# Down projection of a two-layer decoder trunk: seven of eleven row pairs by seven products in all four SwiGLU halves, every second pair's weight sums made by DMA, a larger descriptor store for GpSimd's transfers

## The chip, the cores and the metric

The kernel runs on one core of a Trainium2 chip. The metric is device time in microseconds (us) for one execution; of several executions the median counts. The core has five engines that run in their own order and meet at semaphores: PE (TensorE, matmuls; its weight loads are listed as PEld), DVE (VectorE), ACT (ScalarE), POOL (GpSimd), and SP, which issues most DMAs. [...]

## The reference

Input `x` is 256 tokens by 1024 channels, float32. The trunk has two layers, each of which is: a SwiGLU half step, a mixer (attention), a SwiGLU half step; a final RMSNorm ends it. A half step is

```python
def swiglu(h, w_gate, w_up, w_down):
    return (jax.nn.silu(h @ w_gate) * (h @ w_up)) @ w_down
h = h + 0.5 * swiglu(rmsnorm(h, g), w_gate, w_up, w_down)
```

`w_gate` and `w_up` are 1024 x 2816, `w_down` is 2816 x 1024. There are four such half steps: f10 and f20 in layer 0 (before and after its mixer a), f11 and f21 in layer 1 (before and after its mixer b). The change lies in them.

## The kernel before

**Number format.** Each float32 factor is split into a high part (ScalarE copy into fp32r, tiles `wh`) and a low part (VectorE subtraction, tiles `wl`), and a product is three matmuls: high x high, high x low, low x high (`product`, lines 185 to 192: L188, L190, L192). In the gate and up products of a half step two of the three share one weight load (L199, L205). So every weight that is multiplied passes ACT once and DVE once.

**A half step.** `ffn_blocks` goes over the 22 blocks of 128 hidden channels, two blocks f, f+1 per 1 MB tile of each of `w_gate` and `w_up` (`unit`: load into one of four `raw` buffers by SP, split by ACT L176 and DVE L177 into eight `wh` and eight `wl` buffers). f10's first four blocks are computed by `opening` while the first weights arrive. `close` evaluates silu(gate) x up and keeps each block's activation, split, until the down projection.

**The down projection** (`quartered`) multiplies activations (256 tokens x 2816) by `w_down`. It takes the 22 blocks in 11 pairs 0 to 10. A pair is a 2 x 2 problem: two halves of the tokens (128 each), two blocks of the contraction, two halves of the output (512 columns each).

- A *plain* pair makes all eight products, that is 24 matmuls of 128 x 512.
- A *fast* pair (its number is in `sums`) makes seven products, 21 matmuls, in the manner of Strassen and Winograd (`fast`). It needs four sums of the activations (*left* sums) and four sums of the pair's four weight blocks, a, b, c, d (*right* sums).
- Pairs 9 and 10 are held back and multiplied at the end, output quarter by quarter (`close`).

The left sums are made by `quarter_sums` in the gate and up part, as soon as both blocks of the pair are there: one 256-column and two 128-column VectorE operations (L412 to L414) and a split of the result (ACT L99, DVE L96). They stay in borrowed buffers named in `HOMES`.

The right sums come in one of two ways.

- *By VectorE*: `load` adds in SBUF, one 1024-column operation (tile `sum_..ac`, L655) and two 512-column ones (`sum_..bd`, L656, L657) for each pair. The pair needs one load of 1 MB.
- *By DMA* (pairs in `kept`): `right_sums` lets POOL copy and add rows of `w_down` in HBM, while the gate and up part runs: six calls one after the other, copy a and c, add to both, copy b from a, add, copy d from b, add; each for four pairs in transfers of two pairs (512 KB), 16 transfers in all (L579 copies, L584 adds). Each call is tied to a block of activations by a small POOL copy (L588), so the six are spread over six steps of the loop over f. The pair then needs two raw buffers and 1.75 MB of loads by SP: three of its own blocks and the 1 MB of sums (L640, L641, L643).

In both ways seven weight blocks of 128 x 512 are split by ACT (L633) and DVE (L634), for a plain pair four.

| half step | fast pairs before | of these, sums by DMA | sums by VectorE |
|---|---|---|---|
| f10 | 1 2 4 6 7 | none | 1 2 4 6 7 |
| f20 | 1 to 6 | 1 2 3 4 | 5 6 |
| f11 | 1 2 3 4 6 | 1 2 3 4 | 6 |
| f21 | 1 to 6 | 1 2 3 4 | 5 6 |

**Order of the work.** The program's text gives the data flow; a planner in the framework chooses, when the program is built, the order in which each engine's queue takes its instructions, so that instructions of neighbouring steps are interleaved on DVE and ACT. Each engine then runs its queue strictly in order. The buffers limit how far the supplying engines run ahead of PE: four `raw`, eight `wh` and eight `wl` (a fast pair takes four of each). The tiles `xx0` to `xx3` hold the normalised input of the gate and up part and are free for other use when PE's last gate and up product is done.

**Other names the change touches.** `rotate` (L809 to L817) applies the rotary embedding in the mixers with two temporaries, `rota` and `rotb`, two buffers each. `qkl` holds low parts of queries and keys in the mixers, and the `sum_..ac` tiles in the down projections. `dynamic_dma_scratch_size=1024` (in `kernel`) is the store for descriptors of POOL's transfers.

Of the kernel before, what the change touches and what calls it, by code (L numbers as in the profile page):

```python
# [26 lines left out]
ROT = 16  # L27
# [40 lines left out]
def trunk(ctx: ExitStack, tc: tile.TileContext, a: dict, out: bass.AP):  # L68
    nc = tc.nc
# [112 lines left out]
    def rows(w, k0, k, c0, n):  # L182
        return w[k0 * P:(k0 + k) * P, c0:c0 + n].rearrange("(k p) n -> p k n", p=P)
# [365 lines left out]
    def left_sums(pairs, homes):  # L549

        sums = {}
        assert len(pairs) <= len(homes)
        for i, home in zip(pairs, homes):
            if home in ("mk", "gf"):
                parts = xp.tile([P, 2, 512], F32R, tag=home, name=f"left_{i}")
                sums[i] = (parts[:, 0], parts[:, 1])
            elif home == "qkh":
                parts = ap_.tile([P, 2, 512], F32R, tag=home, name=f"left_{i}", bufs=2)
                sums[i] = (parts[:, 0], parts[:, 1])
            elif home == "pT":  # L560
                sums[i] = tuple(pp.tile([P, 512], F32R, tag=home, name=f"left_{i}_{j}") for j in range(2))
            else:
                sums[i] = tuple(xp.tile([P, 512], F32R, tag=f"{home[:2]}{int(home[2]) + j}", name=f"left_{i}_{j}")
                                for j in range(2))
        return sums

    latest = []

    def right_sums(name, w, first, m, places):


        kept = aside.tile([P, m, 4, 512], F32, tag=f"right_{name}", name=f"right_{name}")
        src = w[2 * first * P:2 * (first + m) * P, :].rearrange("(i k p) (c n) -> k c p i n", k=2, p=P, n=512)
        a, c, d, b = [kept[:, :, j] for j in range(4)]

        def copy(*moves):
            for to, of in moves:
                for i in range(0, m, 2):
                    nc.gpsimd.dma_start(to[:, i:i + 2], of[:, i:i + 2])  # L579

        def add(*moves):
            for to, of in moves:
                for i in range(0, m, 2):
                    nc.gpsimd.dma_start(to[:, i:i + 2], of[:, i:i + 2], accum_op=ALU.add)  # L584

        def paced(call):
            scrap = sp.tile([P, 1], F32, tag="scrap", name="scrap")
            mark = nc.gpsimd.tensor_copy(scrap, latest[-1][:, 0, 0:1].bitcast(F32))  # L588
            with tc.issue_after(mark.ins):
                call()  # L590

        calls = [lambda: copy((a, src[0, 0]), (c, src[1, 1])), lambda: add((a, src[0, 1]), (c, src[0, 1])),
                 lambda: copy((b, a)), lambda: add((b, src[1, 1])), lambda: copy((d, b)), lambda: add((d, src[1, 0]))]
        return {first + i: kept[:, i] for i in range(m)}, {at: lambda call=call: paced(call) for at, call in zip(places, calls)}

    def together(*tables):
        calls = [dict(enumerate(t)) if not isinstance(t, dict) else t for t in tables]

        def run(f):
            for t in calls:  # L600
                if f in t:
                    t[f]()

        return [lambda f=f: run(f) for f in range(KF // 2)]

    def ffn(name, layer, which, norm, after, first=None, beside=(), homes=HOMES, fast=(), queue=(), kept={}, calls={}):
        wg, wu, wd = (a[f"ffn{which}_w_{n}"][layer] for n in ("gate", "up", "down"))
        sums = left_sums(fast, homes)
        blocks = ffn_blocks(name, wg, wu, norm, first, together(beside, calls), sums, queue)
        if which == 1:  # L610
            table(AF.Exp, blocks[-1][:, 0, 0:1].bitcast(F32))
        down(f"{name}_d", wd, blocks, sums, kept, norm.halved(), after)


    def quartered(name, w, acts, sums, kept, collected, tail=2):
# [21 lines left out]
        def load(i):  # L637
            raw = rawp.tile([P, 4, 512], F32, tag="raw", name=f"raw_{name}_{i}")
            if i in kept:
                nc.sync.dma_start(raw[:, :2], rows(w, 2 * i, 2, 0, 512))  # L640
                nc.sync.dma_start(raw[:, 2], w[(2 * i + 1) * P:(2 * i + 2) * P, 512:])  # L641
                right = rawp.tile([P, 4, 512], F32, tag="raw", name=f"raw_{name}_{i}r")
                nc.sync.dma_start(right, kept[i])  # L643
                b11, b21 = split(f"{i}a", raw[:, :2])
                b22, = split(f"{i}b", raw[:, 2:3])
                ta, tc = split(f"{i}c", right[:, :2])
                td, tb = split(f"{i}d", right[:, 2:])
                return b11, b21, b22, ta, tc, tb, td
            nc.sync.dma_start(raw.rearrange("p (k c) n -> p k (c n)", k=2), rows(w, 2 * i, 2, 0, D))
            if i not in sums:  # L650
                return split(f"{i}a", raw[:, :2]) + split(f"{i}b", raw[:, 2:])
            n = sorted(set(sums) - set(kept)).index(i) % 4
            ac = ap_.tile([P, 2, 512], F32, tag="qkl", name=f"sum_{name}_{i}ac", bufs=2)
            bd = xp.tile([P, 2, 512], F32, tag=f"xx{n}", name=f"sum_{name}_{i}bd")
            nc.vector.tensor_add(ac, raw[:, 0::3], raw[:, 1:2].to_broadcast([P, 2, 512]))  # L655
# [151 lines left out]
    def rotate(v, t, name):  # L807

        n = v.shape[1]  # L809
        cs = rot[:, t, 0:1, :].to_broadcast([P, n, ROT])  # L810
        sn = rot[:, t, 1:2, :].to_broadcast([P, n, ROT])
        ta = sp.tile([P, n, ROT], F32, tag="rota", name=f"ra_{name}", bufs=2)
        tb = sp.tile([P, n, ROT], F32, tag="rotb", name=f"rb_{name}", bufs=2)
        nc.vector.tensor_mul(ta, v[:, :, :ROT], cs)
# [189 lines left out]
    n0, n1, n2 = Norm(0, "n0"), Norm(1, "n1"), Norm(2, "n2")  # L1004
    n3, n5, n6 = Norm(4, "n3"), Norm(5, "n5"), Norm(6, "n6")

    kept_f10, calls_f10 = {}, {}
    ffn("f10", 0, 1, n0, n1, first, fast=(1, 2, 4, 6, 7), kept=kept_f10, calls=calls_f10)
    nc.sync.dma_start(rot, a["rot"].rearrange("t p c n -> p t c n"))
    mask = load_mask(0)  # L1010
    xs = n1.xs()
    w, n = a["a_w_qkv"][0], HG * DH
# [7 lines left out]
    def ending(at, apart=2.6):  # L1020
# [3 lines left out]
          [steps(0, 3.0, 11.0, 14.5, 16.5, 19.3), steps(1, 3.0, 11.0, 13.8, 16.5, 19.3), steps(2, 4.0),  # L1024
           [(3.4, "s", (6, 7))] + ending(8.4)],
          a["a_w_o"][0], mask, n2, {3: 4, 4: 5})
    kept_f20, calls_f20 = right_sums("f20_d", a["ffn2_w_down"][0], 1, 4, (1, 2, 3, 4, 5, 6))
    ffn("f20", 0, 2, n2, n3, fast=(1, 2, 3, 4, 5, 6), queue=(6, 7) + (LAST_O,) * 6, kept=kept_f20, calls=calls_f20)
    kx = []
    kept_f11, calls_f11 = right_sums("f11_d", a["ffn1_w_down"][1], 1, 4, (1, 2, 3, 4, 5, 6))  # L1030
    ffn("f11", 1, 1, n3, n5, homes=HOMES[:5], fast=(1, 2, 3, 4, 6),
        beside=[lambda k=k: kx.append(gain(k, 3, "kx", "kx")) for k in range(KD)], kept=kept_f11, calls=calls_f11)
    mask = load_mask(1)
    xkv, xq = by_token(kx), n5.xs()
# [7 lines left out]
          a["b_w_o"][0], mask, n6)  # L1042
    gfin = xp.tile([P, D], F32, tag="gf", name="gfin")
    nc.sync.dma_start(gfin, a["final_norm"].rearrange("(o d) -> o d", o=1).to_broadcast([P, D]))
    kept_f21, calls_f21 = right_sums("f21_d", a["ffn2_w_down"][1], 1, 4, (1, 2, 3, 4, 5, 6))
    sums = left_sums((1, 2, 3, 4, 5, 6), ("mk", "kx4", "kx6", "qkh", "qkh", "pT"))
    h = [[xp.tile([P, 512], F32, tag=f"kx{2 * t + c}", name=f"h_{t}_{c}") for c in range(2)] for t in range(NT)]

    def turn_h(t, c):
        tr = trt(f"h_{t}_{c}")  # L1050
        for k in range(4):
# [5 lines left out]
                        queue=(4, 5, 6, 7) + (LAST_O,) * 4)  # L1057
# [68 lines left out]
```

## Time and profile before

| | |
|---|---|
| time, median of 3 runs (lowest, highest) | 961.97 us (961.61, 962.04) |
| the profiled execution | 962.21 us |
| its span in the trace | 960.4 us |
| granted TensorE clock | 0.999 |
| bytes read from and written to HBM | 208.60 MB, 26.21 MB |

The profile's page has six parts: busy time per engine, the span in 40 slices, DMA queues, the chain of work that ended last, the costliest groups of instructions, and the DMA issues. A group's line gives source line, engine, operation, output<-input, shape and count, then busy time and the mean duration, then the idle time before it and what released it. Timeline rows give the start, the duration, engine and line of an instruction. A row of the view by windows gives a stretch, its length, busy time (and number of instructions) of PE, PEld, DVE, ACT and POOL, the granted clock, the mean busy share of the 16 DMA engines, and GB/s. Durations of successive instructions overlap a little; the distance of starts is what an instruction costs in a full queue.

### The profile page before, as it was taken

What the parts mean: (1) busy time and instruction counts of PE and PEld (TensorE: products, weight loads), DVE (VectorE), ACT (ScalarE), POOL (GpSimd) and SP (SyncE); (2) the same over time, 40 slices, a digit from 0 to 9 for tenths busy, and PEclk for the clock granted to TensorE, in tenths of its full rate; (3) what the DMA queues carried; (4) which work ended last, traced back from release to release, by engine and by line L of the source; (5) the groups of instructions that cost most, each with busy time, mean ns of one, the idle gap of its engine ahead of it and who ended that gap; (6) DMA issues with size and microseconds to landing.
All of it is one profiled execution on the core that took longest, in us unless ns stands there. A gap on an engine that the chain in (4) does not pass through costs nothing.

```text
span 960.4 us, 14716 instructions
## 1 busy us (share of the span) xinstructions
PE 952.6 (99%) x5337; PEld 824.8 (86%) x5337; DVE 802.4 (84%) x1463; ACT 640.6 (67%) x1151; POOL 148.0 (15%) x178
## 2 busy tenths in 40 slices
PE   9999999999999999999999999999999999999997
PEld 7888888888899888888888888888888988888886
DVE  7998889878878888779789986887788789887796
ACT  7866567666867666667586666766577777765661
POOL 0100000022620312100023210000251322120000
PEclk9999999999999999999999999999999999999999
DMA  9785546565235799948849997784624449997661
GB/s 327 245 263 175 177 158 235 201 203 175 93 128 179 256 266 270 318 168 298 260 143 327 276 314 222 273 315 150 245 97 168 132 133 288 262 305 218 232 228 45
DMA packets 138906, 210.61 MB, mean 219 GB/s; under 512 B 4689, under 2 KB 104529, under 8 KB 137297
## 3 DMA queue, kind: packets, MB, share of 16 engines
q1 hardware_dynamic: 128128, 183.58, 56.4%
q0 software_dynamic: 9984, 25.17, 11.5%
q8 instruction: 42, 0.69, 0.3%
q10 hardware_dynamic: 720, 0.92, 0.3%
q14 instruction: 32, 0.25, 0.1%
HBM read 208.60 MB, written 26.21 MB: 244 GB/s over the span
## 4 chain that ended last, share of the span: by engine, by line
PE 98%; DVE 1%; DMA 0%; ACT 0%; issue 0%; POOL 0%; SPq 0%; POOLq 0%; DVEq 0%; ACTq 0%
PE f_g L199 17%; PE f_u L199 17%; PE f_u L205 9%; PE f_g L205 9%; PE dn_f_d L192 6%; PE dn_f_d L190 6%; PE dn_f_d L188 6%; PE dn_f_d_m L192 2%; PE dn_f_d_m L188 2%; PE dn_f_d_m L190 2%; PE qk_a L188 2%; PE qk_a L192 2%; PE qk_a L190 2%; PE v_a L188 1%; PE ot_ao L781 1%; PE ot_ao L783 1%
## 5 line engine op out<-in xcount | busy, mean ns | idle before, releaser
L199 PE MATMUL f_g<-x_n,wh_f_g 128*128 128x512 f32 x672 | 175.8, 393 | 0.0
L199 PE MATMUL f_u<-x_n,wh_f_u 128*128 128x512 f32 x672 | 173.3, 390 | 0.0
L199 PEld LDWEIGHTS f_u<-x_n,wh_f_u 128*128 128x128 f32 x672 | 126.1, 188 | 26.6
L199 PEld LDWEIGHTS f_g<-x_n,wh_f_g 128*128 128x128 f32 x672 | 121.2, 189 | 22.3
L177 DVE TENSOR_TENSOR wl_f_g<-raw_f_g,wh_f_g 128x1024 fp32r<-128x1024 f32 x84 | 101.3, 1219 | 16.9 <-PE f_g L205 15.7
L177 DVE TENSOR_TENSOR wl_f_u<-raw_f_u,wh_f_u 128x1024 fp32r<-128x1024 f32 x84 | 102.5, 1220 | 2.7 <-ACT wh_f_u L176 2.7
L205 PE MATMUL f_u<-x_n,wl_f_u 128*128 128x256 f32 x672 | 101.1, 283 | 0.0
L205 PE MATMUL f_g<-x_n,wl_f_g 128*128 128x256 f32 x672 | 100.5, 282 | 0.0
L205 PEld LDWEIGHTS f_g<-x_n,wl_f_g 128*128 128x128 f32 x672 | 94.2, 190 | 6.1
L176 ACT ACTIVATE wh_f_g<-raw_f_g 128x1024 fp32r<-128x1024 f32 x84 | 87.6, 1052 | 9.1 <-PE f_g L199 5.0
L205 PEld LDWEIGHTS f_u<-x_n,wl_f_u 128*128 128x128 f32 x672 | 89.6, 192 | 0.0
L176 ACT ACTIVATE wh_f_u<-raw_f_u 128x1024 fp32r<-128x1024 f32 x84 | 86.5, 1049 | 2.2 <-PE dn_f_d L192 2.1
L438 ACT ACTIVATE j_f_g<-j_f_g 128x256 f32<-128x256 f32 x88 | 36.2, 417 | 55.0 <-DVE j_f_g L437 53.8
L403 ACT ACTIVATE j_f_g<-f_g 128x256 f32<-128x256 f32 x88 | 33.1, 377 | 27.1 <-PE f_g L205 26.9
L403 ACT ACTIVATE j_f_u<-f_u 128x256 f32<-128x256 f32 x88 | 33.5, 381 | 21.4 <-PE f_u L205 21.3
L301 POOL TENSOR_TENSOR d_n<-w_n,expo 128x8 f32<-128x8 f32 x4 | 7.6, 1898 | 260.4 <-DVE w_n L297 260.4
L584 POOL DMA_DIRECT2D right_f_d<-in_ffn_w_down_dram x24 | 28.0, 1165 | 119.4 <-issue 90.7
L404 DVE TENSOR_TENSOR j_f_g<-f_g,j_f_g 128x256 f32<-128x256 f32 x88 | 37.1, 421 | 7.5 <-ACT j_f_g L403 7.4
L857 POOL TENSOR_SCALAR sm_a<-sm_a,ls_a 128x128 f32<-128x128 f32 (+1 forms) x32 | 32.8, 1044 | 44.1 <-DVE ls_a L855 44.1
L404 DVE TENSOR_TENSOR j_f_u<-f_u,j_f_u 128x256 f32<-128x256 f32 x88 | 37.0, 421 | 0.8 <-ACT j_f_u L403 0.5
L99 ACT ACTIVATE x_n<-gains_hT 128x256 fp32r<-128x256 f32 x48 | 21.7, 500 | 23.6 <-DVE gains_hT L734 23.0
L437 DVE TENSOR_TENSOR j_f_g<-j_f_g,r_n 128x256 f32<-128x256 f32 x88 | 36.5, 421 | 0.4
(690 smaller groups left out, 2369.5 us busy)
## 6 DMA issues: line engine op xcount, KB each, us to landing
raw_f_g<-in_ffn_w_gate_dram SPq DMA_DIRECT2D x42, 1024.0 KB, 5.9
raw_f_u<-in_ffn_w_up_dram SPq DMA_DIRECT2D x42, 1024.0 KB, 6.5
raw_f_d<-in_ffn_w_down_dram SPq DMA_DIRECT2D x32, 1024.0 KB, 6.3
right_f_d<-in_ffn_w_down_dram POOLq DMA_DIRECT2D x36, 512.0 KB, 7.8
raw_qka<-in_a_w_qkv_dram SPq DMA_DIRECT2D x16, 512.0 KB, 4.4
right_f_d<-right_f_d POOLq DMA_DIRECT2D x12, 512.0 KB, 7.7
raw_f_d<-in_ffn_w_down_dram SPq DMA_DIRECT2D x12, 512.0 KB, 4.3
raw_va<-in_a_w_qkv_dram SPq DMA_DIRECT2D x4, 1024.0 KB, 5.7
```

The lines of the kernel that those rows point to most:

```text
L176: nc.scalar.activation(wh, r, AF.Copy)
L177: nc.vector.tensor_sub(wl, r, wh.bitcast(F32))
L188: nc.tensor.matmul(ac, xh, wh, start=first, stop=False)
L190: nc.tensor.matmul(ac, xh, wl, start=False, stop=False)
L192: nc.tensor.matmul(ac, xl, wh, start=False, stop=last)
L199: nc.tensor.matmul(ac, wh, flat(x), start=first and i == 0, stop=False)
L205: nc.tensor.matmul(ac[:, :S], wl, x[:, 0, :], start=False, stop=last and i == len(ws) - 1)
L403: nc.scalar.activation(s, ac[:, S:], AF.Copy)
L404: nc.vector.tensor_add(s, ac[:, :S], s)
L437: nc.vector.tensor_mul(g, g, norm.row)
L438: nc.scalar.activation(g, g, AF.Silu)
L857: nc.gpsimd.tensor_scalar(sm[:, seg], sm[:, seg], ls[:, t:t + 1], None, op0=ALU.mult)
```

## The change

- Pairs 1 to 7 are fast in all four half steps. That makes six plain pairs fast: 3 and 5 in f10, 7 in f20, 5 and 7 in f11, 7 in f21.
- The right sums of pairs 1, 3, 5, 7 come by DMA in all four (`right_sums` with a step of two pairs); those of 2, 4, 6 by VectorE. f10 gets a set of 16 transfers by POOL that it did not have, one step of the loop later than the others (places 2 to 7).
- Both VectorE sums of a pair now lie in `xx` tiles, alternately `xx0`, `xx1` and `xx2`, `xx3`. `qkl` is taken for two left sums in f11 and one in f21.
- `rota` and `rotb` have one buffer each. The descriptor store is 2048 bytes.

```diff
-            elif home == "qkh":
+            elif home in ("qkh", "qkl"):
                 parts = ap_.tile([P, 2, 512], F32R, tag=home, name=f"left_{i}", bufs=2)
...
-    def right_sums(name, w, first, m, places):
+    def right_sums(name, w, first, m, places, step=1):
         kept = aside.tile([P, m, 4, 512], F32, tag=f"right_{name}", name=f"right_{name}")
-        src = w[2 * first * P:2 * (first + m) * P, :].rearrange("(i k p) (c n) -> k c p i n", k=2, p=P, n=512)
+        rows_of = w[2 * first * P:, :].rearrange("(i k p) (c n) -> k c p i n", k=2, p=P, n=512)
+        src = [[rows_of[k, c][:, :(m - 1) * step + 1:step] for c in range(2)] for k in range(2)]
...
-                    nc.gpsimd.dma_start(to[:, i:i + 2], of[:, i:i + 2])
+                    nc.gpsimd.dma_start(to[:, i:min(i + 2, m)], of[:, i:min(i + 2, m)])
...
-        return {first + i: kept[:, i] for i in range(m)}, {at: lambda call=call: paced(call) for at, call in zip(places, calls)}
+        return {first + step * i: kept[:, i] for i in range(m)}, {at: lambda call=call: paced(call) for at, call in zip(places, calls)}
...
-            n = sorted(set(sums) - set(kept)).index(i) % 4
-            ac = ap_.tile([P, 2, 512], F32, tag="qkl", name=f"sum_{name}_{i}ac", bufs=2)
-            bd = xp.tile([P, 2, 512], F32, tag=f"xx{n}", name=f"sum_{name}_{i}bd")
+            n = 2 * (sorted(set(sums) - set(kept)).index(i) % 2)
+            ac, bd = [xp.tile([P, 2, 512], F32, tag=f"xx{n + j}", name=f"sum_{name}_{i}{('ac', 'bd')[j]}") for j in range(2)]
...
-        ta = sp.tile([P, n, ROT], F32, tag="rota", name=f"ra_{name}", bufs=2)
-        tb = sp.tile([P, n, ROT], F32, tag="rotb", name=f"rb_{name}", bufs=2)
+        ta = sp.tile([P, n, ROT], F32, tag="rota", name=f"ra_{name}", bufs=1)
+        tb = sp.tile([P, n, ROT], F32, tag="rotb", name=f"rb_{name}", bufs=1)
...
-    kept_f10, calls_f10 = {}, {}
-    ffn("f10", 0, 1, n0, n1, first, fast=(1, 2, 4, 6, 7), kept=kept_f10, calls=calls_f10)
+    kept_f10, calls_f10 = right_sums("f10_d", a["ffn1_w_down"][0], 1, 4, (2, 3, 4, 5, 6, 7), 2)
+    ffn("f10", 0, 1, n0, n1, first, fast=(1, 2, 3, 4, 5, 6, 7), kept=kept_f10, calls=calls_f10)
...
-    kept_f20, calls_f20 = right_sums("f20_d", a["ffn2_w_down"][0], 1, 4, (1, 2, 3, 4, 5, 6))
-    ffn("f20", 0, 2, n2, n3, fast=(1, 2, 3, 4, 5, 6), queue=(6, 7) + (LAST_O,) * 6, kept=kept_f20, calls=calls_f20)
+    kept_f20, calls_f20 = right_sums("f20_d", a["ffn2_w_down"][0], 1, 4, (1, 2, 3, 4, 5, 6), 2)
+    ffn("f20", 0, 2, n2, n3, fast=(1, 2, 3, 4, 5, 6, 7), queue=(6, 7) + (LAST_O,) * 6, kept=kept_f20, calls=calls_f20)
...
-    kept_f11, calls_f11 = right_sums("f11_d", a["ffn1_w_down"][1], 1, 4, (1, 2, 3, 4, 5, 6))
-    ffn("f11", 1, 1, n3, n5, homes=HOMES[:5], fast=(1, 2, 3, 4, 6),
+    kept_f11, calls_f11 = right_sums("f11_d", a["ffn1_w_down"][1], 1, 4, (1, 2, 3, 4, 5, 6), 2)
+    ffn("f11", 1, 1, n3, n5, homes=HOMES[:5]+("qkl","qkl"), fast=(1, 2, 3, 4, 5, 6, 7),
...
-    kept_f21, calls_f21 = right_sums("f21_d", a["ffn2_w_down"][1], 1, 4, (1, 2, 3, 4, 5, 6))
-    sums = left_sums((1, 2, 3, 4, 5, 6), ("mk", "kx4", "kx6", "qkh", "qkh", "pT"))
+    kept_f21, calls_f21 = right_sums("f21_d", a["ffn2_w_down"][1], 1, 4, (1, 2, 3, 4, 5, 6), 2)
+    sums = left_sums((1, 2, 3, 4, 5, 6, 7), ("mk", "kx4", "kx6", "qkh", "qkh", "pT","qkl","qkl"))
...
-    nc = bacc.Bacc("TRN2", target_bir_lowering=False, num_devices=1, dynamic_dma_scratch_size=1024)
+    nc = bacc.Bacc("TRN2", target_bir_lowering=False, num_devices=1, dynamic_dma_scratch_size=2048)
```

More of the change, by code (lines that the diff above doesn't have):

```diff
@@ L583, in add @@
                 for i in range(0, m, 2):
-                    nc.gpsimd.dma_start(to[:, i:i + 2], of[:, i:i + 2], accum_op=ALU.add)
+                    nc.gpsimd.dma_start(to[:, i:min(i + 2, m)], of[:, i:min(i + 2, m)], accum_op=ALU.add)
         def paced(call):
@@ L590, in paced @@
                 call()
-        calls = [lambda: copy((a, src[0, 0]), (c, src[1, 1])), lambda: add((a, src[0, 1]), (c, src[0, 1])),
-                 lambda: copy((b, a)), lambda: add((b, src[1, 1])), lambda: copy((d, b)), lambda: add((d, src[1, 0]))]
-        return {first + i: kept[:, i] for i in range(m)}, {at: lambda call=call: paced(call) for at, call in zip(places, calls)}
+        calls = [lambda: copy((a, src[0][0]), (c, src[1][1])), lambda: add((a, src[0][1]), (c, src[0][1])),
+                 lambda: copy((b, a)), lambda: add((b, src[1][1])), lambda: copy((d, b)), lambda: add((d, src[1][0]))]
+        return {first + step * i: kept[:, i] for i in range(m)}, {at: lambda call=call: paced(call) for at, call in zip(places, calls)}
     def together(*tables):
```

## The prediction, on record before the result was known

> **What bounds the kernel now.** I read the page's busy times and its chain of work first, then PE's own waits.
>
> ```profile
> span 960.4 us, 14716 instructions
> PE 952.6 (99%) x5337; PEld 824.8 (86%) x5337; DVE 802.4 (84%) x1463; ACT 640.6 (67%) x1151; POOL 148.0 (15%) x178
> ...
> PE 98%; DVE 1%; DMA 0%; ACT 0%; issue 0%; POOL 0%; SPq 0%; POOLq 0%; DVEq 0%; ACTq 0%
> ```
>
> ```profile
> PE busy L124 <- PEq L1109: 0.8, 1, 0.8
> PE f_g L199 <- ACT wh L483: 0.4, 1, 0.4
> ```
>
> PE carries 98% of the chain that ended last, and in the whole execution it waited for another engine twice, 1.2 us in all. So a matmul taken away is time taken away, as long as nothing begins to wait. What one costs I read from the down projection of f20, by windows of exactly one pair: pair 2 (fast, sums by DMA), pair 5 (fast, sums by VectorE), pair 7 (plain).
>
> ```profile
> 432.21:436.97 4.76, 4.76 (x23) 3.94 (x22) 4.33 (x5) 3.71 (x4) 0.00 (x0) 1.00 0.99 397
> 446.49:451.25 4.76, 4.76 (x23) 3.94 (x22) 4.69 (x7) 2.29 (x3) 0.00 (x0) 1.00 0.44 151
> 456.01:461.45 5.44, 5.44 (x26) 4.50 (x25) 5.44 (x7) 5.16 (x7) 0.00 (x0) 1.00 1.03 337
> ```
>
> A fast pair takes 4.76 us for 21 matmuls, a plain one 5.44 us for 24: 0.227 us each way, at a granted clock of 1.00, whether DVE is busy for 4.33 or 4.69 us and whether the DMA engines are 44% or 99% busy. (The counts in the rows include a matmul that reaches in from the neighbouring pair.)
>
> [...]
>
> **The change, part by part.**
>
> *Removed from PE.* Six plain pairs become fast (two in f10, one in f20, two in f11, one in f21): 6 x (5.44 - 4.76) = 6 x 0.68 = 4.08 us. Nothing is added to PE.
>
> *Left sums of six more pairs*, in the gate and up parts. The groups of instructions by line:
>
> ```profile
> L412 DVE TENSOR_TENSOR q_f<-act_f 128x256 f32<-128x256 f32 x22 | 9.3, 422 | 0.0
> L413 DVE TENSOR_TENSOR q_f<-q_f,act_f 128x128 f32<-128x128 f32 x22 | 6.3, 288 | 0.1
> L414 DVE TENSOR_TENSOR q_f<-act_f,q_f 128x128 f32<-128x128 f32 x22 | 6.3, 288 | 0.0
> L96 DVE TENSOR_TENSOR left<-q_f,left 128x512 fp32r<-128x512 f32 x22 | 15.2, 692 | 2.9 <-ACT left L99 2.6
> ```
>
> One pair costs DVE 0.42 + 0.29 + 0.29 + 0.69 = 1.69 us. Gate and up of f10 (from its second loop step on), f20 and f11 by windows:
>
> ```profile
> 39.69:128.77 89.08, 89.08 (x513) 78.74 (x513) 76.97 (x142) 55.58 (x104) 0.00 (x0) 1.00 0.57 189
> 321.96:422.18 100.22, 100.22 (x577) 88.55 (x577) 83.53 (x153) 64.69 (x118) 17.78 (x22) 1.00 0.90 265
> 497.00:602.00 105.00, 105.00 (x606) 92.81 (x605) 89.47 (x166) 69.27 (x126) 20.84 (x25) 1.00 0.92 273
> ```
>
> DVE has 12.1 us free in f10 and 15.5 us in f11, and gets 3.4 us more in each; f20 gets 1.7 us. They lie beside matmuls and cost nothing on the path. Without that cover they would cost 10.1 us.
>
> *Right sums by VectorE*, now pairs 2, 4 and 6 of each down projection. DVE works off pair 6 of f20 in these steps (first sum; last split; first split of pair 7), and PE uses that last split here; below, the same for f21, with the one wait there for a load:
>
> ```profile
> 445.75 1.22 DVE L655 TENSOR_TENSOR sum_f_d_6ac<-raw_f_d 128x1024 f32<-128x1024 f32 x1
> ...
> 451.12 1.22 DVE L634 TENSOR_TENSOR wl_f_d_6d<-sum_f_d_6bd,wh_f_d_6d 128x1024 fp32r<-128x1024 f32 x1
> 452.26 1.22 DVE L634 TENSOR_TENSOR wl_f_d_7a<-raw_f_d,wh_f_d_7a 128x1024 fp32r<-128x1024 f32 x1
> ```
>
> ```profile
> 454.87 0.39 PE L190 MATMUL dn_f_d_m<-wl_f_d_6d,left 128*128 128x512 f32 x1
> ...
> 930.66 0.39 PE L190 MATMUL dn_f_d_m<-wl_f_d_6d,left 128*128 128x512 f32 x1
> ```
>
> ```profile
> 915.04 1.23 DVE L655 TENSOR_TENSOR sum_f_d_5ac<-raw_f_d 128x1024 f32<-128x1024 f32 x1 [1.12 <-DMA raw_f_d<-in_ffn_w_down_dram]
> ...
> 927.90 1.23 DVE L634 TENSOR_TENSOR wl_f_d_6d<-sum_f_d_6bd,wh_f_d_6d 128x1024 fp32r<-128x1024 f32 x1
> ```
>
> A pair with VectorE sums takes DVE 452.26 - 445.75 = 6.51 us against PE's 4.76: DVE loses 1.75 us of its lead. A pair with DMA sums takes DVE 4.33 us and gains 0.43. The lead at pair 6's last split is 454.87 - 452.34 = 2.53 us in f20 and 930.66 - 929.13 = 1.53 us in f21, after two VectorE pairs in a row. After the change there are three by then, each followed by a DMA pair. Taken against the old order, the third costs 1.75 and the DMA pair behind it returns 0.43: leads of 1.2 us in f20 and 0.2 us in f21. That is the low side; f10 and f11 get f20's order. On the high side, DVE's own idle time absorbs the third pair (it stood still 1.12 us in f21 for a load) and the leads stay at 2.5. Either way PE does not wait; I take nothing. With the cover gone, a lead below zero is paid by PE in full, because everything behind the waiting matmul is PE's own queue. The first VectorE pair's sums now wait for `xx`, that is for the end of gate and up; PE then has pairs 0 and 1 to do, 5.44 + 4.76 = 10.2 us, against 6.51 us on DVE.
>
> *Loads in the down projection.* Four DMA pairs in a row asked for 1.84 MB each per 4.76 us, 385 GB/s, about all that the row above shows (397). Alternating, two pairs ask for 2.88 MB in 9.52 us, 303 GB/s. The total is unchanged in f20, f11 and f21; f10 gets 4 x 0.79 MB more. I take nothing, and expect f21's wait of 1.12 us to vanish.
>
> *The new set of DMA sums in f10.* Chain of the set in f20: POOL's first copies, the last two adds, their landing; and where f10 stands:
>
> ```profile
> 322.05 2.33 POOL L579 DMA_DIRECT2D right_f_d<-in_ffn_w_down_dram  x3
> ...
> 387.52 1.16 POOL L584 DMA_DIRECT2D right_f_d<-in_ffn_w_down_dram  x1 [0.77 <-DMA right_f_d<-right_f_d]
> 397.91 1.17 POOL L584 DMA_DIRECT2D right_f_d<-in_ffn_w_down_dram  x1 [9.23 <-issue]
> ```
>
> ```profile
> DMA to landing us min/median/max: 4.1/7.7/10.1
> ```
>
> ```profile
> 39.45 0.72 ACT L99 ACTIVATE act_f<-act_f 128x256 fp32r<-128x256 f32 x2
> ```
>
> ```profile
> 128.59 0.40 PE L188 MATMUL dn_f_d<-wh_f_d_0a,act_f 128*128 128x512 f32 x1
> ```
>
> ```profile
> raw_f_d_1r<-right_f_d SPq DMA_DIRECT2D x3, 1024.0 KB, 6.3
> ```
>
> From the first copy, sums of the first half of the pairs have landed after 387.5 + 7.7 - 322.0 = 73 us, of the second half after 84 us. In f10 the first call hangs on the blocks of 39.45, so it starts at 40.2; the halves are there at 113 and 124. The down projection starts at 128.6, pair 1's sums are multiplied 7.5 us later (pair 0 and nine matmuls), and their load (6.3 us) and splits (2.3 us) come before: the load must be issued by 127.5, or 124 if pair 2's load, queued behind it on SP (2.6 us at 397 GB/s), is to be early too. Slack: 11 us. Cost: nothing.
>
> *Descriptors 2048 bytes.* POOL stands still between two adds, with nothing else named:
>
> ```profile
> POOL right_f_d L584 <- issue: 90.7, 14, 9.2
> ```
>
> If that is room for descriptors, more transfers fly at once, and the weights' loads in gate and up land later. For f20's `raw_f_u`, and a load of `w_gate` with the split that takes it:
>
> ```profile
> DMA to landing us min/median/max: 5.2/9.2/12.9
> ```
>
> ```profile
> 335.52 0.37 SPq L167 DMA_DIRECT2D raw_f_g<-in_ffn_w_gate_dram  x1
> ```
>
> ```profile
> 351.95 1.05 ACT L176 ACTIVATE wh_f_g<-raw_f_g 128x1024 fp32r<-128x1024 f32 x1
> ```
>
> 16.4 us from issue to split, 12.9 at worst for the landing, and the eight `wh` hold two more loop steps of 11.1 us each ahead of PE. If loads took twice the worst, 25.8 us, the split would slip by 9.4 us inside these: nothing. A gain it can't be either, POOL isn't waited for.
>
> *One buffer for `rota`, `rotb`.* The four operations are DVE's, in order, so a second buffer can't let them overlap:
>
> ```profile
> L814 DVE TENSOR_TENSOR ra_a<-rt_a,rot x8: 285/293/534, 198.9 to 257.6; 128x128 f32<-128x128 f32 x8
> ```
>
> If each of 18 calls (ten more in mixer b) waited a whole such operation, DVE would lose 18 x 0.29 = 5 us in two mixers of over 110 us where it is busy for about 80%. Nothing; at worst inside the range.
>
> *Sum.* The profiled execution took 962.21 us, 1.81 outside its span. 960.4 - 4.08 = 956.3 of span, 958.1 with what lies around it. The median was 0.24 below that execution: **957.9 us**.
>
> **The rivals.**
>
> *A. DVE runs out of lead.* One landing wait of f21's kind (1.12 us) in each down projection, on top of the low-side leads (1.2, 1.2, 1.2, 0.2): PE would wait 0 to 0.1 in three and 0.9 in f21. If the planner's new order costs DVE another 0.3 each (one 128 x 256 operation ahead of the split), 0.2 x 3 + 1.2 = 1.8 us, so 959.7. For it: leads of 1.5 to 2.5 us are thin. Against it: f10 ran five VectorE pairs without a wait of PE, and alternating lets DVE recover.
>
> *B. No change.* PE's pace is set by something that the removed matmuls do not touch, or waits eat the 4 us: 962.0. Against it the equal pace of all pairs.
>
> *C. Slower: f10's DMA sums come late.* DMA in f10's stretch: 0.57 x 89.08 = 50.8 us; one set of POOL's transfers takes a third of
>
> ```profile
> q0 software_dynamic: 9984, 25.17, 11.5%
> ```
>
> or 0.115 x 960.4 / 3 = 36.8 us. Together 87.6 of 89.1 us: full, where f20 still has a tenth free. If the 16 transfers each took the 10.1 us of the slowest instead of 7.7, the first half would land 0.31 x 73 = 22.8 us later, 12 us beyond the slack, and SP's queue would hold the other loads behind that one: 957.9 + 12 = 970. It decides against the change from 11 + 4.1 = 15 us of delay, a chain a fifth longer. Against it: POOL's waits say that the chain is as long as it is for lack of room, and the room doubles.
>
> **How the numbers follow.** Forecast 68%, A 17%, B 7%, C 8%. The forecast's own range is 957.4 to 958.6 (other parts at zero, 0.3 us of scatter between runs and up to 0.7 of small waits). For eight in ten I add A and some of its neighbourhood: 957.3 to 960.3; C and B lie outside. 0.2% of the time is 1.9 us, about what can be told from no change, so faster means below 960.05: the forecast and most of A, 82%; same 10%; slower 8%.
>
> **What would show it.** PE's matmuls fall by 18 (some records may be missing), each of pairs 1 to 7 takes 4.76 us in all four down projections, and PE's waits stay near 1.2 us. A shows as waits of PE's L188 or L190 for DVE or ACT of pairs 4 to 7, C as a load of sums in f10 that SP issues after 124 us. POOL's idle time before L584 shows whether the descriptor store was the limit. I am wrong if the gate and up parts get longer, or if PE waits over 2 us.

## The result, and the profile after

| | before | changed |
|---|---|---|
| time, median (lowest to highest), 5 runs each | 961.97 us (961.55 to 962.32) | 968.1 us (966.52 to 972.09) |
| ratio to before, 95% interval | | 1.0075 (1.0061 to 1.0090) |
| profiled execution, its span | 962.21, 960.4 us | 966.52, 964.7 us |

The changed kernel is slower by 0.75%, outside the predicted range. It also scatters by 5.6 us, where before scattered by 0.8; the profiled execution is its fastest, so the losses read from it are the small ones.

The page of the changed kernel: span, busy times, POOL's DMA queue, the chain that ended last, and the split of `w_up` on ACT.

```profile
span 964.7 us, 14828 instructions
...
PE 951.5 (99%) x5319; PEld 822.2 (85%) x5319; DVE 820.1 (85%) x1505; ACT 641.0 (66%) x1169; POOL 163.8 (17%) x200
...
q0 software_dynamic: 13312, 33.56, 15.5%
...
PE 83%; DMA 7%; DVE 4%; ACT 3%; issue 2%; POOL 0%; ACTq 0%; POOLq 0%; SPq 0%; DVEq 0%
...
L176 ACT ACTIVATE wh_f_u<-raw_f_u 128x1024 fp32r<-128x1024 f32 x84 | 87.2, 1050 | 26.7 <-DMA raw_f_u<-in_ffn_w_up_dram 26.2
```

PE lost exactly the 18 matmuls (5337 to 5319), yet the chain is PE's for 83% only, where it was 98%: loads of weights now stand in it, and ACT waited 26.2 us for loads of `w_up`. PE's own waits:

```profile
PE f_u L199 <- DVE j_f_g L404: 5.4, 2, 3.6
PE busy L124 <- PEq L1109: 0.8, 1, 0.8
PE qt_a L953 <- DVE rt_a L817: 0.2, 1, 0.2
```

Where the time went is seen when the execution is cut at the first matmul of each part (from PE's rows in the timelines; us). The last two columns are experiments 1 and 5 below.

| part | before | changed | 1024 bytes | 1024 bytes, two buffers |
|---|---|---|---|---|
| f10 gate and up | 123.90 | 129.35 | 123.71 | 123.64 |
| f10 down | 57.38 | 56.01 | 56.01 | 56.21 |
| mixer a | 113.38 | 113.81 | 113.91 | 113.37 |
| f20 gate and up | 122.63 | 122.62 | 122.63 | 122.63 |
| f20 down | 56.69 | 56.02 | 56.02 | 56.01 |
| f11 gate and up | 123.49 | 125.53 | 123.48 | 123.49 |
| f11 down | 57.36 | 56.29 | 56.00 | 56.00 |
| mixer b | 113.78 | 113.79 | 113.74 | 113.76 |
| f21 gate and up | 124.46 | 124.64 | 124.47 | 124.48 |
| f21 down, to its last matmul | 55.82 | 55.14 | 55.14 | 55.14 |

The four down parts give back 3.79 of the predicted 4.08 us. f10's gate and up part loses 5.45 us, f11's 2.04, mixer a 0.43, f21's gate and up 0.18. The rest of this section follows the largest, in f10.

POOL's queue in the changed kernel's f10 (start, duration): the copies of the first call, then the adds of the second.

```profile
40.36 3.02 POOL L580 DMA_DIRECT2D right_f_d<-in_ffn_w_down_dram  x4
...
51.25 3.57 POOL L585 DMA_DIRECT2D right_f_d<-in_ffn_w_down_dram  x3
60.30 1.13 POOL L585 DMA_DIRECT2D right_f_d<-in_ffn_w_down_dram  x1 [5.47 <-issue]
```

Three adds go out back to back, where before one went out every 8 to 10 us (in f20 at 332.15, 341.41, 349.52 and 358.56). A load of 1 MB of `w_up` is issued by SP in the middle of them. The chain of waits, in order of time (start, duration):

```profile
52.80 17.88 DMA raw_f_u<-in_ffn_w_up_dram
...
72.97 3.27 PE f_u L199 x8
76.24 1.35 PE f_g L205 x8
...
80.38 1.81 PE f_u L199 x8
82.20 0.95 PE f_g L205 x8
```

It landed after 17.9 us. The same load took 5.3 us before, and ACT took it for splitting 7.0 us after its issue:

```profile
52.84 0.37 SPq L167 DMA_DIRECT2D raw_f_u<-in_ffn_w_up_dram  x1
...
59.88 1.99 ACT L176 ACTIVATE wh_f_u<-raw_f_u 128x1024 fp32r<-128x1024 f32 x2
```

Now ACT, DVE and PE in the changed kernel, each in the order of its own queue:

```profile
59.11 1.05 ACT L176 ACTIVATE wh_f_g<-raw_f_g 128x1024 fp32r<-128x1024 f32 x1
70.76 1.06 ACT L176 ACTIVATE wh_f_u<-raw_f_u 128x1024 fp32r<-128x1024 f32 x1 [10.60 <-DMA raw_f_u<-in_ffn_w_up_dram]
71.72 0.40 ACT L99 ACTIVATE act_f<-act_f 128x256 fp32r<-128x256 f32 x1
72.03 0.36 ACT L403 ACTIVATE j_f_g<-f_g 128x256 f32<-128x256 f32 x1
```

```profile
60.40 1.22 DVE L177 TENSOR_TENSOR wl_f_u<-raw_f_u,wh_f_u 128x1024 fp32r<-128x1024 f32 x1
72.16 0.42 DVE L96 TENSOR_TENSOR act_f<-act_f,act_f 128x256 fp32r<-128x256 f32 x1 [10.54 <-ACT act_f L99]
72.50 0.42 DVE L404 TENSOR_TENSOR j_f_g<-f_g,j_f_g 128x256 f32<-128x256 f32 x1
```

```profile
67.32 2.00 PE L199 MATMUL f_g<-x_n,wh_f_g 128*128 128x512 f32 x8
72.97 3.27 PE L199 MATMUL f_u<-x_n,wh_f_u 128*128 128x512 f32 x8 [3.65 <-DVE j_f_g L404]
```

ACT came to the split at 60.2 and stood until 70.8. Behind it in ACT's queue stood L403, which reads a finished accumulator out; DVE's L404, the other half of the reading, stood behind DVE's wait for ACT. So accumulators were not emptied, and PE, which had its weights, stopped for want of an accumulator: the releaser of its 3.65 us is L404. And the matmuls after the gap ran slower: eight of L199 in 3.27 us and eight of L205 in 1.35, against 1.81 and 0.95 in the next block, 1.86 us more. 3.65 + 1.86 = 5.5 us is f10's loss. (Durations overlap a little in a full queue; by distances of starts PE is 3.8 us late and then 1.7 us slower, the same sum.) Three windows of 2 us behind the gap show the granted clock (the number ahead of the last two, which are the DMA share and GB/s):

```profile
72.90:74.90 2.00, 1.93 (x6) 1.55 (x7) 2.00 (x5) 1.13 (x3) 1.09 (x2) 0.68 1.11 351
74.90:76.90 2.00, 2.00 (x9) 1.71 (x8) 2.00 (x3) 0.68 (x3) 0.00 (x0) 0.50 1.05 406
76.90:78.90 2.00, 2.00 (x16) 1.91 (x16) 2.00 (x7) 1.23 (x3) 0.00 (x0) 0.97 1.02 332
```

In the two windows after the gap the granted clock is 0.68 and 0.50 (1.00 in the last 2 us of the gap), and in the third it is back at 0.97.

### The profile page after: what moved, and what is told of

It reads as the page before. It is cut to its first block, busy times and chain, and to the rows that moved or that the text cites. A ratio compares the mean times of both kernels' runs of the same rounds, so it can differ in the third digit from the quotient of the medians.

```text
span 964.7 us, 14828 instructions
## 1 busy us (share of the span) xinstructions
PE 951.5 (99%) x5319; PEld 822.2 (85%) x5319; DVE 820.1 (85%) x1505; ACT 641.0 (66%) x1169; POOL 163.8 (17%) x200
## 3 DMA queue, kind: packets, MB, share of 16 engines
q0 software_dynamic: 13312, 33.56, 15.5%
## 4 chain that ended last, share of the span: by engine, by line
PE 83%; DMA 7%; DVE 4%; ACT 3%; issue 2%; POOL 0%; ACTq 0%; POOLq 0%; SPq 0%; DVEq 0%
PE f_u L199 13%; PE f_g L199 13%; PE f_g L205 7%; PE f_u L205 7%; DMA raw_f_u<-in_ffn_w_up_dram 5%; PE dn_f_d L192 4%; PE dn_f_d L188 4%; PE dn_f_d L190 4%; PE dn_f_d_m L192 2%; PE dn_f_d_m L188 2%; PE dn_f_d_m L190 2%; PE qk_a L188 2%; PE qk_a L192 1%; PE qk_a L190 1%; DVE wl_f_u L177 1%
## 5 line engine op out<-in xcount | busy, mean ns | idle before, releaser
L199 PE MATMUL f_u<-x_n,wh_f_u 128*128 128x512 f32 x672 | 174.9, 392 | 5.4 <-DVE j_f_g L404 5.4
L199 PE MATMUL f_g<-x_n,wh_f_g 128*128 128x512 f32 x672 | 175.9, 393 | 0.1
L199 PEld LDWEIGHTS f_u<-x_n,wh_f_u 128*128 128x128 f32 x672 | 126.6, 189 | 33.2 <-DVE j_f_g L404 6.5
L199 PEld LDWEIGHTS f_g<-x_n,wh_f_g 128*128 128x128 f32 x672 | 121.2, 189 | 22.6 <-DVE j_f_u L404 0.3
L176 ACT ACTIVATE wh_f_u<-raw_f_u 128x1024 fp32r<-128x1024 f32 x84 | 87.2, 1050 | 26.7 <-DMA raw_f_u<-in_ffn_w_up_dram 26.2
L205 PE MATMUL f_u<-x_n,wl_f_u 128*128 128x256 f32 x672 | 101.1, 283 | 0.0
L205 PE MATMUL f_g<-x_n,wl_f_g 128*128 128x256 f32 x672 | 100.9, 283 | 0.0
L205 PEld LDWEIGHTS f_g<-x_n,wl_f_g 128*128 128x128 f32 x672 | 94.8, 191 | 6.2
L205 PEld LDWEIGHTS f_u<-x_n,wl_f_u 128*128 128x128 f32 x672 | 89.6, 192 | 0.0
L404 DVE TENSOR_TENSOR j_f_g<-f_g,j_f_g 128x256 f32<-128x256 f32 x88 | 37.0, 420 | 31.0 <-ACT j_f_g L403 30.9
L99 ACT ACTIVATE act_f<-act_f 128x256 fp32r<-128x256 f32 x56 | 22.9, 411 | 33.9 <-DVE act_f L447 33.9
L96 DVE TENSOR_TENSOR act_f<-act_f,act_f 128x256 fp32r<-128x256 f32 x56 | 23.5, 422 | 24.5 <-ACT act_f L99 24.5
L585 POOL DMA_DIRECT2D right_f_d<-in_ffn_w_down_dram x32 | 37.6, 1470 | 26.2 <-issue 26.2
L589 POOL COPY scrap<-act_f 128x1 f32<-128x1 f32 x24 | 13.9, 579 | 162.6 <-ACT act_f L99 162.6
L404 DVE TENSOR_TENSOR j_f_u<-f_u,j_f_u 128x256 f32<-128x256 f32 x88 | 36.8, 418 | 0.5 <-ACT j_f_u L403 0.5
L857 POOL TENSOR_SCALAR sm_b<-sm_b,ls_b 128x128 f32<-128x128 f32 (+1 forms) x32 | 29.8, 957 | 43.0 <-DVE ls_b L855 43.0
```

What stands on the lines that cost most here:

```text
L96: return first, nc.vector.tensor_sub(lo, src, hi.bitcast(F32))
L176: nc.scalar.activation(wh, r, AF.Copy)
L199: nc.tensor.matmul(ac, wh, flat(x), start=first and i == 0, stop=False)
L205: nc.tensor.matmul(ac[:, :S], wl, x[:, 0, :], start=False, stop=last and i == len(ws) - 1)
L404: nc.vector.tensor_add(s, ac[:, :S], s)
L585: nc.gpsimd.dma_start(to[:, i:min(i + 2, m)], of[:, i:min(i + 2, m)], accum_op=ALU.add)
```

## The experiments

Theory R (room): 2048 bytes for descriptors put several adds in flight, and they slow the weights' loads. Theory T (traffic): f10's new set of transfers is too much for its DMA queues, whatever the room.

**1. The descriptor store alone undone.**

```diff
-    nc = bacc.Bacc("TRN2", target_bir_lowering=False, num_devices=1, dynamic_dma_scratch_size=2048)
+    nc = bacc.Bacc("TRN2", target_bir_lowering=False, num_devices=1, dynamic_dma_scratch_size=1024)
```

> The changed kernel with the descriptor store back at 1024 bytes; all else as changed. Theory R (room): the 2048 bytes let three adds of POOL fly at once, and the weights' loads beside them land after 17.9 us (f10) and up to 22.2 us (f11) instead of 12.9 at most; ACT waits for them in order, the accumulators behind ACT are not emptied, and PE stops. With one add at a time no load takes over 14 us, PE's waits fall back to some 1.2 us, f10's gate and up part is 123.9 us again (it was 129.35), f11's 123.5 (was 125.5), and the time is 957.9 (957.3 to 958.8), the sum of the prediction. Theory T (traffic): f10's new set of 16 transfers is too much for its DMA queues whatever the room; then f10 stays 3 to 6 us longer and the time is 961 to 964, with only f11's 2 us returned.

Measured: 958.67 us (958.27 to 959.93), ratio 0.9969 (0.9957 to 0.9981). The same place in POOL's queue, how long the load of `w_up` beside it took, and PE's waits:

```profile
51.49 1.21 POOL L585 DMA_DIRECT2D right_f_d<-in_ffn_w_down_dram  x1 [0.34 <-issue]
60.53 1.17 POOL L585 DMA_DIRECT2D right_f_d<-in_ffn_w_down_dram  x1 [7.83 <-issue]
```

```profile
DMA to landing us min/median/max: 10.1/10.1/10.1
```

```profile
PE busy L124 <- PEq L1109: 0.8, 1, 0.8
PE f_g L199 <- ACT wh L483: 0.3, 1, 0.3
PE qt_a L953 <- DVE rt_a L817: 0.2, 1, 0.2
```

One add at a time, the load lands after 10.1 us, and f10 and f11 have their old lengths. T falls: all of f10's traffic is there. The kernel is now faster than before.

**2. The descriptor store alone done**, in the kernel before (with one buffer for `rota` and `rotb`, to make room).

```diff
-        ta = sp.tile([P, n, ROT], F32, tag="rota", name=f"ra_{name}", bufs=2)
-        tb = sp.tile([P, n, ROT], F32, tag="rotb", name=f"rb_{name}", bufs=2)
+        ta = sp.tile([P, n, ROT], F32, tag="rota", name=f"ra_{name}", bufs=1)
+        tb = sp.tile([P, n, ROT], F32, tag="rotb", name=f"rb_{name}", bufs=1)
...
-    nc = bacc.Bacc("TRN2", target_bir_lowering=False, num_devices=1, dynamic_dma_scratch_size=1024)
+    nc = bacc.Bacc("TRN2", target_bir_lowering=False, num_devices=1, dynamic_dma_scratch_size=2048)
```

> The kernel before with a store of 2048 bytes (and one buffer for rota and rotb, which makes the room). Theory R: the three sets it has (f20, f11, f21) now issue three adds at once, loads of gate and up land late as in the changed kernel, and it gets slower: by about 2 us in f11, nothing to 2 in f20 and f21, so 962.5 to 966, and more scatter between runs. Theory T: nothing changes, 962.0 (961.6 to 962.4); the buffers of rota cost nothing under both.

Measured: 962.41 us (961.94 to 962.97), ratio 1.0005 (0.9996 to 1.0014): hardly more than nothing, and below what R expected. PE's waits sum to 1.2 us, as before. Yet loads of `w_up` in f11 landed late here too (the latest after 22.2 us in the changed kernel):

```profile
DMA to landing us min/median/max: 5.4/10.0/20.1
```

So loads that are late by this much do not suffice. f10 has no set of transfers here. Mixer a is 113.81 us long here too, 0.43 more than before, which is about all of the difference.

**3. f10 as before, the rest changed.**

```diff
-    kept_f10, calls_f10 = right_sums("f10_d", a["ffn1_w_down"][0], 1, 4, (2, 3, 4, 5, 6, 7), 2)
-    ffn("f10", 0, 1, n0, n1, first, fast=(1, 2, 3, 4, 5, 6, 7), kept=kept_f10, calls=calls_f10)
+    kept_f10, calls_f10 = {}, {}
+    ffn("f10", 0, 1, n0, n1, first, fast=(1, 2, 4, 6, 7), kept=kept_f10, calls=calls_f10)
```

> The changed kernel, store of 2048 bytes, but f10 as it was before: five fast pairs, all sums by VectorE, no DMA sums. Four of the six new fast pairs remain: -2.7 us. Theory R: f10's 5.5 us come back, f11 keeps its 2 us: about 961.5 (960.5 to 964, scattered). Theory T: the loss was f10's set alone: 959.3 to 960.3.

Measured: 963.17 us (961.0 to 966.07), ratio 1.0015 (1.0005 to 1.0025). f10's gate and up part is 123.2 us; f11's is 124.8, with a wait of PE of 1.2 us, in the fastest execution. This is R's case (960.5 to 964) and not T's (959.3 to 960.3): f10's time is back, and what is left still loses, by the median, more than the 2.7 us that its four new fast pairs bring (4.08 x 4/6).

**4. A store between.**

```diff
-    nc = bacc.Bacc("TRN2", target_bir_lowering=False, num_devices=1, dynamic_dma_scratch_size=2048)
+    nc = bacc.Bacc("TRN2", target_bir_lowering=False, num_devices=1, dynamic_dma_scratch_size=1536)
```

> The changed kernel with a store of 1536 bytes. Theory R: POOL issues two adds back to back instead of three, so the loads beside them land late by less: f10's gate and up part between 123.9 and 129.35 us and the time between that of 1024 bytes and 968, say 958.5 to 963. Theory T: as with 2048 bytes or 1024, within 1 us of both.

Measured: 965.56 us (963.32 to 967.32), ratio 1.0033 (1.0021 to 1.0044). POOL issued the adds of the second call as two, one, one; the load in question landed after

```profile
DMA to landing us min/median/max: 13.5/13.5/13.5
```

and f10's gate and up part is 125.4 us, f11's 125.7. The time lies between the two, as R has it, but above the 958.5 to 963 that I had expected: room for a second add already costs most of it. The next two loads in f10, issued 3.6 and 8.9 us after that one, took 20.1 and 17.8 us here, against 17.3 and 14.9 in the changed kernel, so the number of adds in flight does not by itself give a load's time.

**5. Two buffers for the rotation, on top of 1.**

```diff
-        ta = sp.tile([P, n, ROT], F32, tag="rota", name=f"ra_{name}", bufs=1)
-        tb = sp.tile([P, n, ROT], F32, tag="rotb", name=f"rb_{name}", bufs=1)
+        ta = sp.tile([P, n, ROT], F32, tag="rota", name=f"ra_{name}", bufs=2)
+        tb = sp.tile([P, n, ROT], F32, tag="rotb", name=f"rb_{name}", bufs=2)
```

> The changed kernel with 1024 bytes for descriptors and two buffers again for rota and rotb. Both kernels with one buffer and an undisturbed trace show mixer a 0.4 to 0.5 us longer than before (113.91 and 113.81 us against 113.38), with a wait of PE for the rotation of 0.24 us. Theory B (the buffer costs it): mixer a is 113.4 us again, that wait is gone, and the time is 0.4 to 0.5 us below that of 1024 bytes alone, 958.2 (957.7 to 958.5). Rival: the planner's order, changed by something else, costs it; then 958.7 and the wait stays.

Measured: 957.98 us (957.7 to 959.59), ratio 0.9963 (0.9951 to 0.9976), the lowest median of all, though its interval overlaps that of experiment 1. Mixer a is 113.37 us, and PE's waits are one row:

```profile
PE busy L124 <- PEq L1109: 0.8, 1, 0.8
```

The traces show that the buffer does cost: mixer a takes 113.8 to 113.9 us in all eight with one buffer, and 113.4, 113.4 and 113.6 in the three with two (before, 5 and 9). DVE's queue at the first rotation in mixer a, in the kernel before (two buffers) and in experiment 1 (one):

```profile
200.51 0.29 DVE L817 TENSOR_TENSOR rt_a<-ra_a,rb_a 128x128 f32<-128x128 f32 x1
200.71 0.28 DVE L814 TENSOR_TENSOR ra_a<-rt_a,rot 128x128 f32<-128x128 f32 x1
```

```profile
198.95 0.29 DVE L817 TENSOR_TENSOR rt_a<-ra_a,rb_a 128x128 f32<-128x128 f32 x1
199.16 1.22 DVE L387 TENSOR_TENSOR wl_qka<-raw_qka,wh_qka 128x1024 fp32r<-128x1024 f32 x1
200.29 0.29 DVE L814 TENSOR_TENSOR ra_a<-rt_a,rot 128x128 f32<-128x128 f32 x1
```

With one buffer the planner puts a split of 1.13 us between two rotations that followed each other; the second rotation is later by that, and PE's transposes wait for it (the 0.2 us in the waits of 1). The other 0.2 to 0.3 us is in no row of the waits.

**6. f11 as before, the rest changed, 2048 bytes.**

```diff
-    kept_f11, calls_f11 = right_sums("f11_d", a["ffn1_w_down"][1], 1, 4, (1, 2, 3, 4, 5, 6), 2)
-    ffn("f11", 1, 1, n3, n5, homes=HOMES[:5]+("qkl","qkl"), fast=(1, 2, 3, 4, 5, 6, 7),
+    kept_f11, calls_f11 = right_sums("f11_d", a["ffn1_w_down"][1], 1, 4, (1, 2, 3, 4, 5, 6))
+    ffn("f11", 1, 1, n3, n5, homes=HOMES[:5], fast=(1, 2, 3, 4, 6),
```

> The changed kernel, 2048 bytes, with f11 alone as before: five fast pairs, the first four with DMA sums. The kernel before with 2048 bytes had loads landing after 20.1 us in f11 too, and PE did not wait there. Theory R with slack: the two more pairs of left sums put ACT and DVE behind, so that the same late load reaches PE; then f11's gate and up part is 123.5 us here, with loads still landing near 20 us, its down part 57.4. Rival (chance of the hour): PE waits 1 to 2 us in f11 all the same, 124.5 to 125.5. In both f10 loses its 2 to 6 us, and the time is 965 to 970.

Measured: 966.73 us (two runs, 965.71 and 967.75). f11's gate and up part is 123.35 us and no wait of PE lies in it, though loads of `w_up` took up to

```profile
DMA to landing us min/median/max: 5.4/10.1/19.6
```

This was meant to answer 2: in f11, loads of some 20 us reach PE with seven fast pairs and not with five. But the loads are not equally late. Two loads of `w_up` in each trace's f11, issued some 31.5 and 41.7 us into it (us from issue to landing), and PE's wait, in one execution of each:

| run | fast pairs in f11 | first load | second load | wait of PE |
|---|---|---|---|---|
| experiment 2 | five | 10.8 | 20.1 | none |
| experiment 6 | five | 9.9 | 19.6 | none |
| changed | seven | 17.6 | 22.2 | 1.75 |
| experiment 3 | seven | 18.3 | 21.6 | 1.17 |
| experiment 4 (1536 bytes) | seven | 17.2 | 22.3 | 1.85 |

With seven fast pairs the first load is late too, and the second lands 1.5 to 2.7 us later, which is the size of the waits. The experiment also put f11's DMA sums back on pairs 1 to 4 in a row, so it changed two things. At 1024 bytes, with seven fast pairs each, the first load took 10.3 us with the sums in a row (experiment 7) and 14.7 with every second pair (experiment 1), and PE did not wait: which rows the transfers touch is a rival cause of the lateness. That the left sums take slack which a late load needs is not shown. In f20 and f21 of the changed kernel, also with seven fast pairs, loads of `w_up` took up to 20.2 and 21.4 us and PE did not wait for them.

f10, with its new set, lost its time here as well (130.5 us, with one stop of PE of 3.97 us).

**7. DMA sums for pairs 1 to 4, VectorE's for 5, 6, 7**, at 1024 bytes; the same edit in all four.

```diff
-    kept_f20, calls_f20 = right_sums("f20_d", a["ffn2_w_down"][0], 1, 4, (1, 2, 3, 4, 5, 6), 2)
+    kept_f20, calls_f20 = right_sums("f20_d", a["ffn2_w_down"][0], 1, 4, (1, 2, 3, 4, 5, 6))
...
-    nc = bacc.Bacc("TRN2", target_bir_lowering=False, num_devices=1, dynamic_dma_scratch_size=2048)
+    nc = bacc.Bacc("TRN2", target_bir_lowering=False, num_devices=1, dynamic_dma_scratch_size=1024)
```

> The changed kernel with 1024 bytes, but the DMA sums for pairs 1 to 4 in a row and VectorE's for 5, 6, 7 in a row in all four down projections. By the leads of the prediction: a lead of 5.8 us at pair 4, less 1.75 for each VectorE pair, leaves 0.6 us at pair 7, less 1.1 for a load that lands late: PE waits 0 to 1 us in each down part, 958.7 to 962. Rival: DVE's idle time absorbs it, all four down parts stay at 56.0, 56.0, 56.0, 55.1 us, and the order of the pairs is worth nothing: 958.7.

Measured: 960.76 us (959.48 to 962.14), 2.1 us above experiment 1 by the medians; the two ratios, 0.9989 (0.9979 to 0.9998) and 0.9969 (0.9957 to 0.9981), touch at their edges. In its profiled execution f10's down part is 56.48 and f21's 56.07 us (56.01 and 55.14 when alternating), while f20's and f11's are as in experiment 1. In f21 PE waits for a split that DVE made late:

```profile
PE dn_f_d L190 <- DVE wl_f_d_9b L635: 0.6, 1, 0.6
```

So in two of the four the lead does run out, in the size that the leads gave (0 to 1 us in each).

**8. Copies in place of adds, 2048 bytes.**

```diff
-                    nc.gpsimd.dma_start(to[:, i:min(i + 2, m)], of[:, i:min(i + 2, m)], accum_op=ALU.add)
+                    nc.gpsimd.dma_start(to[:, i:min(i + 2, m)], of[:, i:min(i + 2, m)])
```

> The changed kernel, 2048 bytes, with plain copies in place of the adding transfers (POOL's 32 adds in HBM are left out: the right sums of pairs 1, 3, 5, 7 are single blocks). As many transfers of the same size fly at once, or more. [...] Theory R2 (it is the number of transfers in the second queue, whatever they do): loads still land after 17 to 22 us, and the time is 962 to 968.

Measured: 958.55 us (958.11 to 958.92), ratio 0.9967 (0.9955 to 0.9979); PE waits for no load. (With the adds left out this kernel's sums are single blocks; it serves for its time alone.) The load of f10 took

```profile
DMA to landing us min/median/max: 13.4/13.4/13.4
```

and the slowest later ones 16.8 to 17.6. R2 falls by its time, 962 to 968 us, though the slowest loads reach the low end of its 17 to 22: with as many transfers, all of them copies, the kernel takes what experiment 1 takes (958.67). Four copies at once delay loads too (13.4 us in f10, against 5.3 before), but less than three adds (17.9), and short of PE. In f10 the DMA engines moved 334 GB/s from 50 to 70 us here and 247 in the changed kernel, at the same busy share (1.03 and 1.06). POOL's queue shows 33.56 MB in both, here in fewer packets and less of the engines' time.

```profile
q0 software_dynamic: 9216, 33.56, 11.1%
```

64 copies in 9216 packets are 144 each; with 32 copies and 32 adds in 13312, an add has 272. By estimate from the two shares (11.1% of 956.3 us and 15.5% of 964.7) a copy took 1.7 us of all 16 engines and an add 3.0. Whether the bytes in the profile are all that an add moves is not shown, so 247 against 334 GB/s does not tell that the engines got less done beside adds.

**9. f10's DMA sums left to VectorE**, on top of 5.

```diff
-    kept_f10, calls_f10 = right_sums("f10_d", a["ffn1_w_down"][0], 1, 4, (2, 3, 4, 5, 6, 7), 2)
+    kept_f10, calls_f10 = {}, {}
```

> The changed kernel with 1024 bytes and two buffers for rota and rotb, but f10 without a set of DMA sums: its seven fast pairs all get their sums from VectorE. This prices the set that f10 got. By the prediction's rates DVE loses 1.75 us of lead for each of seven pairs, 12.3 us in all, against a lead of some 7 us at the start: PE would wait 3 to 6 us in f10's down part, which becomes 59 to 62 us instead of 56.0, and the time 961 to 964. Rival: in e7 three such pairs in a row cost less than their 5.25 us, because DVE had idle time to give; then f10's down part is 56 to 57.5 us and the set saves little: 958 to 959.5.

Measured: 964.63 us (964.39 to 964.75), ratio 1.0029 (1.0018 to 1.0040); f10's down part is 62.5 us, both a little above what I had expected. PE waits for splits of the sums:

```profile
PE dn_f_d_m L188 <- ACT wh_f_d_5d L634: 0.8, 1, 0.8
PE dn_f_d_m L188 <- ACT wh_f_d_7d L634: 0.8, 1, 0.8
...
PE dn_f_d_m L188 <- ACT wh_f_d_5c L634: 0.7, 1, 0.7
PE dn_f_d_m L188 <- ACT wh_f_d_7c L634: 0.6, 1, 0.6
```

These show 2.9 of 6.3 us. The distances of PE's starts in pairs 3 to 7 show 6.1: the four waits are 3.6 so, and some twenty more matmuls start 0.1 to 0.25 us late, which the view does not list. f10's set of DMA sums is worth 964.63 - 957.98 = 6.65 us: with seven fast pairs it has to be there.

## Why the prediction was wrong

**PE sets the end, six pairs are worth 4.08 us: right.** 18 matmuls fewer, and in experiment 1 down parts of 56.0, 56.0, 56.0 and 55.1 us, 4.08 less than before. With the store and the rotation undone the sum came true: 957.98 measured, 957.9 predicted. The rival that PE's pace is set by something else falls with it.

**Right sums by VectorE, loads alternating: right.** No down part of experiments 1 and 5 has a wait of PE; experiment 7 shows the lead running out in f10 and f21 when the order does not alternate, and experiment 9 what it costs without the DMA pairs.

**"Descriptors 2048 bytes ... nothing": this step failed**, in three places. (That the store was the limit was right: POOL's idle time before its adds fell from 90.7 to 26.2 us.)
- It took the time from issue to split from one load in f20, 16.4 us. In f10 ACT came for the load of 52.80 at 60.2, 7.4 us later. The kernel before already showed 7.0 us at this place, with a load of 5.3 us: 1.7 us were to spare. Slack had to be read in each part, at its tightest load.
- It let a late split slip "inside" the two loop steps that the eight `wh` hold ahead of PE. Those protect PE's weights. But the split waits at the head of ACT's queue, and behind it stands the emptying of accumulators, which lasted PE for 9 us here (60.2 to 69.3), not for two steps. I named who waits for POOL and not who waits behind ACT. A load of 17.9 us, well under the 25.8 that I had called harmless, cost 5.5 us.
- It priced the lateness at 12.9 us of the old kernel times two, without asking what more adds in flight do. At this load, one gave 10.1 us, two 13.5, three 17.9.

**Left sums "lie beside matmuls and cost nothing": right while loads are on time** (experiments 1 and 5 have no wait of PE in a gate and up part beyond the first matmuls). Beside late loads PE did wait in f11, 1.2 to 1.9 us; whether the left sums have a part in that, or only the later loads, stays open (experiment 6).

**One buffer for the rotation "nothing": wrong, by 0.2 to 0.5 us.** DVE does make the operations one after the other, as its rows in experiment 5 show; but the buffer also binds the planner, which could no longer set two rotations next to each other as it had.

**The rivals.** C had the place (f10, its DMA engines busy for 0.96 of the time from 30 to 130 us, against 0.60 before) and the sign, not the mechanism: no load of sums was late for PE; its weights' loads were. A did not show in the changed kernel's profiled execution; in that of experiment 6, whose f20 is the same, PE waited 0.5 us for a split of f20's pair 6, and the part took 56.8 us.

The loss after the gap was in no step: behind a stall of 3.65 us slower matmuls cost another 1.7 us. The granted clock is 0.68 and 0.50 in the next two windows of 2 us there, and after experiment 6's 3.97 us it is 0.50, 0.50 and 0.53 in three. After f11's 1.75 us it stays at 1.00 (548 to 552 us), and eight matmuls took 2.11 us with their modelled end, against 1.98 undisturbed. How long a stall has to be for the clock to fall is not shown.

What stays open: why the changed kernel scatters up to 972.09 us. Only its fastest execution has a trace; that the others have more or longer stalls of this kind fits experiments 1 and 8, whose scatter is 1.7 and 0.8 us, and is not shown. The two slowest runs do have the lowest granted clock, 0.993 and 0.994 against 0.996 in the profiled one; by estimate 0.003 of 965 us is 2.9 of the 5.6 us.

## What to carry to other kernels

When a resource that throttles a background queue is enlarged, ask what the throttle protected: here one add at a time left POOL idle for 90.7 us before its adds (the kernel before) and let a load land after 10.1 us (experiment 1), where three made it 17.9. A late load costs what stands behind the instruction that waits for it, so follow that engine's queue down to the next thing PE needs, which may be an empty accumulator and not a weight. Take slack where it is smallest, and test the parts of a change one by one: two of its edits, which cost 10 us between them and looked like housekeeping, hid a gain of 4.

## What the runs showed of the hardware

- Three adds in HBM by DMA slowed a load at one place in f10 more than four copies of the same size did. That load of 1 MB took 5.3 us with no transfer of POOL beside it, 10.1 with one add in flight, 13.5 with two, 17.9 with three, 13.4 with four copies. The next two loads do not follow that order: 20.1 and 17.8 us with two adds (experiment 4), 17.3 and 14.9 with three.
- How many of POOL's transfers of 512 KB went out back to back grew with the descriptor store: with 1024 bytes three copies or one add, with 1536 two adds, with 2048 three. A copy has 144 packets (9216 for 64 in experiment 8), an add 272 (13312 for 32 of each in the changed kernel).
- A stall of PE of 3.65 us cost some 1.7 us more in slower matmuls after it, one of 3.97 us (experiment 6) some 2.8; stalls of 1.2 to 1.9 us cost 0.1 to 0.4 us beyond themselves (f11's gate and up part against 123.5 us; changed, experiments 3 and 4).
